# Summing the four partial modulation rows on TensorE and adding their bias on ScalarE

## The chip, the cores and the metric

One core of a Trainium2 chip runs the whole program. The metric is the device time of one execution in microseconds (us). The engines are TensorE (PE, with its weight loads as PEld), VectorE (DVE), ScalarE (ACT), GpSimd (POOL) and SyncE (SP); SP and ACT issue most DMAs from their queues. Each engine carries out its own instructions in program order and waits on semaphores for the others.

## The reference, cut to what matters

Two layers of a hybrid block. Each is steered by six modulation vectors of 1024 per stream (`l` the latents, `c` the context), which come out of one product of a conditioning vector with `w_mod`:

```python
silu_c = jax.nn.silu(c)
silu_cc = jax.nn.silu(c_ctx)
for i in range(DEPTH):            # 2 layers
    ...
    mod_l = jnp.split((silu_c @ w_mod[i] + b_mod[i])[:, None, :], 6, axis=-1)
    mod_c = jnp.split(silu_cc @ w_mod[i] + b_mod[i], 6, axis=-1)
    h_l = modulate(rmsnorm(x, norm_mix_g[i]), mod_l[0], mod_l[1])
    ...
    y_l, y_c = hybrid_mixer(h_l, h_c, p, ctx_out)
    x = x + mod_l[2] * y_l
    x = x + mod_l[5] * expert_choice_ffn(modulate(rmsnorm(x, norm_ffn_g[i]), mod_l[3], mod_l[4]), ...)
    ...
```

`w_mod` is 1024 x 6144 in each layer. `hybrid_mixer` has four branches (attention, an SSD scan, an S5 scan, a short convolution) with gates; `expert_choice_ffn` has 16 experts.

## The kernel before

The 6144 columns of a layer are taken in 24 chunks of 256, so there are 48 chunks in all. `mods` makes one chunk at a time. The contraction of 1024 is split over four column groups of TensorE: the 8 products of L191 leave four partial sums in one PSUM bank (`ps`), group q on rows 32q and 32q+1, one row for each stream. ScalarE copies the bank to `row` in SBUF (L194). What follows is finishing work:

- Two transposes by TensorE (L199) put the chunk's 256 columns onto the partitions, in the first half of a second PSUM bank (`pb`, seen as `pt`).
- VectorE adds the four partial sums (L201, a reduction into `modT`) and then the bias `bmT` (L202).
- Chunks of the parts 2 and 5 are gate chunks, 16 of the 48. The gates are also wanted as rows in DRAM (`mrow`). For them a product with `sel` (L206), a 128 x 32 matrix whose column s has ones on the rows 32q+s, adds the partial sums as rows into the other half of the same bank (`pr`). It is written after L201 in the program, and writes the bank that L201 reads. A DMA from ACT's queue brings the bias rows into `br` (L208; one buffer only, so it waits until the store before has read it), VectorE adds them (L209), for part 5 it also halves them (L212), and SP's queue stores the result to `mrow` (L213).
- Chunks of the parts 1 and 4 make `a_mix` or `a_ffn` by VectorE (L219). This stays.

`mods` is called in the mixer's normalisation (chunks 0 to 7 of layer 0, L355), and in `branches`: as a side generator of the filler work that `main` makes (chunks 8 to 23 of layer 0 and 0 to 7 of layer 1 in layer 0; chunks 16 to 23 of layer 1 in layer 1), and in a run of its own for chunks 8 to 15 of layer 1 (L395). The dense products of the filler (L98 to L100, on `hH`, `hL`, `fwH`, `fwL`) and these chunks share the PSUM banks called `psmm`. The branches SSD and S5 have chains of short steps on DVE, POOL, ACT and PE in banks called `psa` and `psb`; a scheduler interleaves filler and chains by priority, once, when the program is built. At run time each engine's order is fixed. The part of S5's chain that matters here: VectorE builds powers and tables (L986 to L991, into `lo`, `hi`, `Cx`, `z`), then for each group it runs a scan (L1176), combines it into `g` and `S` (L1183 to L1187), and TensorE multiplies that (L1192, L1194).

Of the kernel before, what the change touches and what calls it, by code (L numbers as in the profile page):

```python
# [15 lines left out]
OP = mybir.AluOpType  # L16
# [12 lines left out]
# columns of the packed constants  # L29
# [8 lines left out]
# columns of a layer's packed small parameters  # L38
# [20 lines left out]
class Kern:  # L59
    def __init__(self, ctx, tc, I, out):  # L60
        self.ctx, self.tc, self.nc, self.I, self.out = ctx, tc, tc.nc, I, out
        self.uid = 0
        self.early, self.wafter = (2, 7), {}
        # the experts' weight slots past the early ones: the pools they lie in, bottom up, and the order of first use
        self.lay = ((6, 4, 1, 1), (4, 3, 2, 3))
        self.turn = ([2] + [0] * 6 + [3] + [1] * 4, [2] * 2 + [0] * 4 + [3] * 3 + [1] * 3)

    # ---------------------------------------------------------------- small helpers
# [9 lines left out]
    def psum(self, a, b, mm):  # L78
        """the PSUM banks: for two chains of steps and for the dense products"""
# [6 lines left out]
    def va(self, n, tag=None):  # L86
        """a PSUM bank for a branch's chain of steps"""
# [3 lines left out]
    def pa(self, n):  # L91
        """a PSUM bank for the dense products"""
        return self.va(n, "mm")
# [8 lines left out]
    def split(self, pool, tag, shape, x, bufs=None):  # L102
        """x in two parts that fp32r products carry"""
# [13 lines left out]
    def rsqrt(self, pool, out, x, scale, eps, n, short=False):  # L117
        """out = (x * scale + eps) ** -0.5 on [128, n]"""
# [18 lines left out]
    def constants(self, pool, first, last):  # L137
        """a run of the packed constants"""
# [5 lines left out]
    # ---------------------------------------------------------------- set-up  # L144
    def setup(self):
# [29 lines left out]
        # the experts' inputs and affinities, by layer and stream  # L175
# [3 lines left out]
    def mods(self, l, js, pool=None):  # L179
        """chunks of 256 of layer l's adaLN rows: modT [128, part*8, stream]; the gates' rows to DRAM.  # L180
        Four column groups take two of the eight contraction blocks each"""
# [4 lines left out]
        for j in js:  # L186
# [8 lines left out]
            yield  # L195
            pb = self.pa(512)
            pt = pb[:, :256].rearrange("p (b q c) -> p b q c", b=2, q=4)
            for b in range(2):
                nc.tensor.transpose(pt[:, b].rearrange("p q c -> p (q c)"), row[:, b * 128:(b + 1) * 128], self.ident)  # L199
            mv = modT[:, 2 * j:2 * j + 2]  # L200
            nc.vector.tensor_reduce(mv, pt[:, :, :, 0:2].rearrange("p b q s -> p b s q"), axis=AX.X, op=OP.add)  # L201
            nc.vector.tensor_add(mv, mv, self.bmT[:, l, 2 * j:2 * j + 2, None].to_broadcast([128, 2, 2]))  # L202
            part, jj = divmod(j, 4)
            if part in (2, 5):
                pr = pb[:32, 256:]
                nc.tensor.matmul(pr, self.cst["sel"], row, start=True, stop=True, skip_group_check=True)  # L206
                br = st.tile([2, 256], F32, name="br", tag="br", bufs=1)
                nc.scalar.dma_start(br, I["bmr"][l, part // 3, :, jj * 256:(jj + 1) * 256])  # L208
                nc.vector.tensor_add(br, br, pr[:2])  # L209
                if part == 5:  # L210
                    # the experts' hidden values come twice: halved here
                    nc.vector.tensor_scalar(br, br, 0.5, None, op0=OP.mult)  # L212
# [10 lines left out]
    # ---------------------------------------------------------------- weights and dense products  # L223
    def fraw(self, src, n, pool=None):
        """half of the contraction blocks of a chunk of weights"""
# [4 lines left out]
    def wload(self, src, k, n, extra=None):  # L230
        """weights src [k*128, n] split to fp32r parts: a list of blocks; more columns may be appended"""
# [28 lines left out]
    def cm(self, w, m, o, n):  # L260
        """channel-major product: [128 channels (m-th of the chunk), tokens o..o+n]"""
# [5 lines left out]
    def tm(self, w, t, n):  # L267
        """token-major product: [128 tokens of tile t, n columns]"""
# [5 lines left out]
    # ---------------------------------------------------------------- mixer  # L274
# [21 lines left out]
    def wchunks(self, l):  # L296
        """the experts' weights in the order of use, a quarter of a matrix at a time"""
        n = 0
        for e in range(16):
            for nm in ("w_exp_gate", "w_exp_up", "w_exp_down"):  # L300
                for h in range(4):
# [4 lines left out]
                    if (l, e, nm) == (1, 15, "w_exp_down"):  # L306
                        # the last products go by quarters of the columns
# [10 lines left out]
    def norm(self, l):  # L318
        nc, L0 = self.nc, l == 0
        with self.pool("np") as np_:  # L320
# [24 lines left out]
            if L0:  # L345
                rows = []
                for q in range(5):
                    if q == 3:
                        # the first products take each block as soon as it is there
# [53 lines left out]
    def gate(self, b, mc):  # L403
        """tanh of half a quarter of a branch's gates, kept in DRAM"""
# [10 lines left out]
    def merge(self, l):  # L415
        """the sum of the gated branches onto the residual, then the experts' inputs, tile by tile"""
# [6 lines left out]
        # the experts' weights: the first slots are there from here on, the others once the mixer is done  # L423
# [6 lines left out]
        with self.pool("mg") as mg, ExitStack() as right:  # L430
            mH, mL = (mg.tile([128, 8, W], F32R, name="m" + p) for p in "HL")
            with self.pool("ya") as ya, self.pool("mrg") as mp:
                merged = mp.tile([128, 8, W], F32, name="merged")

                def lower(n):
                    """the lower parts of all but the last n sums"""
# [65 lines left out]
            def add(w, t, c):  # L502
                """a quarter of the columns of a tile"""
# [17 lines left out]
            # the router works on the rows before they are normalised and modulated: its weights take the scale,  # L521
            # the shift gives a row of its own
# [62 lines left out]
    # ---------------------------------------------------------------- short convolution  # L585
# [9 lines left out]
    def pos(o):  # L595
        """column of token o in the padded layout"""
        return o + 1 if o < 256 else o + 3

    def conv(self, dst, xp, w, b):
        """dst[:, i] = w0 x[i] + w1 x[i+1] + w2 x[i+2] (+ b), 770 wide"""  # L600
# [34 lines left out]
    # ---------------------------------------------------------------- SSD  # L635
    def ssd(self):
# [3 lines left out]
        # half the convolution's weights, for silu(y) = (tanh(y/2) + 1) * y/2  # L640
# [42 lines left out]
        # step sizes  # L683
        v = wp.tile([128, NT, 2, 8], F32, name="dtv", tag="dt0")
        for hf, ex in ((1, C_DT), (0, None)):
            w = self.win(C_Z + hf * 256, 256, ex)
            for t in range(NT):
# [7 lines left out]
                if t in self.tiles:  # L695
                    # z, silu'd (twice)
# [929 lines left out]
```

## Time and profile before

| | |
|---|---|
| time, median of 3 runs | 3142.2 us (3141.09 to 3142.49) |
| span of the profiled execution | 3138.9 us |
| its own time | given by its span; the median of the timed runs lies 3.3 us above |
| TensorE busy | 2878.1 us, 92% |
| VectorE busy | 1600.4 us, 51% |
| ScalarE busy | 789.8 us, 25% |
| GpSimd busy | 547.0 us, 17% |

The span runs from the first to the last instruction that the profiler recorded on the one core; the timed runs also hold what lies around it. The busy shares are means over stages with different limits.

### The profile page before, as it was taken

The page shows a single profiled execution, that of the slowest core. Times are in us where ns is not written, and L with a number is a line of the kernel's source. Part 1 is how long each engine was busy: PE and PEld are TensorE (multiplying, and loading weights), DVE is VectorE, ACT ScalarE, POOL GpSimd, SP SyncE. Part 2 cuts the span into 40 slices and gives each one's busy share as a digit, 9 for nine tenths or more (in the row PEclk, how much of TensorE's full clock was granted, in tenths as well). Part 3 has the DMA queues.
Part 4 walks back from the last instruction along what each step waited for, and adds up shares of the span by engine and source line. Part 5 has one row for each costly group of instructions (what it writes and reads, how often), then busy time and mean ns, then how long its engine had stood idle before and what let it go on. Part 6 is the DMA issues. An engine that isn't in the chain of part 4 may idle for free. (4 is left out here: it accounts for less than half of the span.)

```text
span 3138.9 us, 47411 instructions
## 1 busy us (share of the span) xinstructions
PE 2878.1 (92%) x18866; PEld 1863.1 (59%) x18866; DVE 1600.4 (51%) x3581; ACT 789.8 (25%) x1733; POOL 547.0 (17%) x623
## 2 busy tenths in 40 slices
PE   7999888999999979999999799977999996998887
PEld 4866766787788944444443476756686785332223
DVE  5467688555326652323232546798865565232223
ACT  4253222335422200000000332322435421000001
POOL 1022266100004120101000104065210031010001
PEclk9999989999999989999999899988999997999999
DMA  7324433401356369898887541432320486999997
GB/s 235 114 69 133 136 99 121 130 33 35 107 171 207 132 251 384 341 350 342 343 341 280 169 122 54 152 105 74 95 78 18 155 287 252 409 408 409 409 409 302
DMA packets 319615, 648.27 MB, mean 207 GB/s; under 512 B 21409, under 2 KB 190625, under 8 KB 319394
## 3 DMA queue, kind: packets, MB, share of 16 engines
q1 hardware_dynamic: 300688, 601.66, 53.1%
q10 hardware_dynamic: 15186, 32.93, 2.8%
q0 software_dynamic: 3520, 10.65, 0.9%
q8 instruction: 149, 2.44, 0.3%
q14 instruction: 72, 0.59, 0.1%
HBM read 599.71 MB, written 42.32 MB: 205 GB/s over the span
## 5 line engine op out<-in xcount | busy, mean ns | idle before, releaser
L1329 PE MATMUL psa<-we,X 128*64 128x512 f32 (+1 forms) x4096 | 591.8, 492 | 31.1 <-DMA we<-in_w_exp_gate_dram 15.5
L1329 PEld LDWEIGHTS psa<-we,X 128*64 128x64 f32 (+1 forms) x4096 | 203.1, 124 | 394.9 <-issue 285.8
L98 PE MATMUL psmm<-hH,fwH 128*128 128x512 f32 x984 | 373.0, 379 | 8.4 <-DVE xpad L628 3.6
L100 PE MATMUL psmm<-hH,fwL 128*128 128x512 f32 x984 | 368.7, 375 | 0.0
L99 PE MATMUL psmm<-hL,fwH 128*128 128x512 f32 x984 | 367.2, 373 | 0.0
L1359 PE MATMUL psa<-we,hidT 128*64 128x512 f32 x992 | 244.4, 608 | 18.0 <-ACT hidT L1347 11.5
L98 PEld LDWEIGHTS psmm<-hH,fwH 128*128 128x128 f32 x984 | 189.9, 193 | 55.4 <-issue 16.9
L100 PEld LDWEIGHTS psmm<-hH,fwL 128*128 128x128 f32 x984 | 189.9, 193 | 34.7 <-issue 7.8
L99 PEld LDWEIGHTS psmm<-hL,fwH 128*128 128x128 f32 x984 | 189.9, 193 | 31.8 <-issue 6.6
L1340 ACT ACTIVATE hid<-psa 128x512 f32<-128x512 f32 (+1 forms) x48 | 25.3, 526 | 718.3 <-PE psa L1329 574.8
L1364 DVE SCALAR_TENSOR_TENSOR y<-psa,ag,m 64x512 f32<-64x512 f32 x62 | 46.5, 750 | 241.8 <-PE psa L1359 241.0
L1359 PEld LDWEIGHTS psa<-we,hidT 128*64 128x64 f32 x992 | 70.7, 138 | 159.4 <-issue 118.9
L114 DVE TENSOR_TENSOR fwL<-fr,fwH 128x1024 fp32r<-128x1024 f32 (+1 forms) x100 | 115.8, 1159 | 92.9 <-ACT fwH L113 84.0
L1320 POOL TENSOR_TENSOR X<-X,modT 128x512 f32<-128x512 f32 x40 | 41.2, 1042 | 679.2 <-DVE X L1319 679.1
L1342 DVE TENSOR_TENSOR hid<-hid,psa 128x512 f32<-128x512 f32 (+1 forms) x48 | 28.7, 597 | 236.0 <-PE psa L1329 235.7
L465 POOL TENSOR_TENSOR merged<-merged,tgm 128x512 f32<-128x512 f32 (+1 forms) x48 | 62.6, 1323 | 472.3 <-DVE tgm L463 472.0
L113 ACT CAST fwH<-fr 128x1024 fp32r<-128x1024 f32 (+1 forms) x100 | 89.4, 896 | 133.7 <-PE psmm L99 70.3
L98 PE MATMUL psa<-cwH,hH 128*128 128x256 f32 (+1 forms) x432 | 122.4, 284 | 0.2
L100 PE MATMUL psa<-cwH,hL 128*128 128x256 f32 (+1 forms) x432 | 121.7, 282 | 0.0
L99 PE MATMUL psa<-cwL,hH 128*128 128x256 f32 (+1 forms) x432 | 121.4, 281 | 0.0
L1341 DVE SCALAR_TENSOR_TENSOR hid<-hid,psa 128x512 f32<-128x512 f32 (+1 forms) x48 | 28.7, 597 | 165.8 <-ACT hid L1340 165.8
L410 ACT ACTIVATE tg<-psmm 128x512 f32<-128x512 f32 x96 | 50.9, 530 | 169.0 <-PE psmm L100 150.4
(527 smaller groups left out, 5965.8 us busy)
## 6 DMA issues: line engine op xcount, KB each, us to landing
we<-in_w_exp_gate_dram SPq DMA_DIRECT2D x128, 1024.0 KB
we<-in_w_exp_up_dram SPq DMA_DIRECT2D x128, 1024.0 KB
we<-in_w_exp_down_dram SPq DMA_DIRECT2D x128, 1024.0 KB
fr<-in_w_mod_dram SPq DMA_DIRECT2D x96, 512.0 KB
fr<-in_w_in_dram SPq DMA_DIRECT2D x64, 512.0 KB
raw<-in_w_in_dram SPq DMA_DIRECT2D x36, 512.0 KB
gs<-tg ACTq DMA_DIRECT2D x32, 384.0 KB
tgm<-gs SPq DMA_DIRECT2D x32, 384.0 KB
```

Source lines behind the costliest of these rows:

```text
L98: self.nc.tensor.matmul(ps, ah, bh, start=start and i == 0, stop=False)
L99: self.nc.tensor.matmul(ps, ah, bl, start=False, stop=False)
L100: self.nc.tensor.matmul(ps, al, bh, start=False, stop=stop and i == n - 1)
L113: self.nc.scalar.copy(h, x)
L114: self.nc.vector.tensor_sub(l, x, h.bitcast(F32))
L410: nc.scalar.activation(tg[:, o:o + n], self.cm(w, m, o, n), AF.Tanh, scale=0.5)
L465: (V if i == 3 else nc.gpsimd).tensor_add(dst, dst, t)
L1320: nc.gpsimd.tensor_add(X[:, hk], X[:, hk], Bm[:, 24 + h * 4:28 + h * 4, s:s + 1].to_broadcast([128, 4, 128]))
L1329: self.lastup = nc.tensor.matmul(ps[s][j * c:(j + 1) * c], X[s][:, k, r:r + c], w(k)[:, j * n:(j + 1) * n], start=k == 0, stop=k == 7, ski ...
L1341: V.scalar_tensor_tensor(hid, hid, 1.0, g, op0=OP.add, op1=OP.mult)
L1359: nc.tensor.matmul(ps[j * c:(j + 1) * c], lh, w(k)[:, j * n:(j + 1) * n], start=k == 0, stop=k == 7, skip_group_check=True)
L1364: V.scalar_tensor_tensor(Y[s][r, nn], ps[j * c:(j + 1) * c], got[s][1][r, e:e + 1], m5[s][r, nn], op0=OP.mult, op1=OP.mult)
```

## The change

The four partial sums are no longer transposed and then reduced. Two products with `row` as the stationary and the first two columns of `sel` as the moving operand (new L208) transpose and add at once, into 2 x 2 columns of PSUM. ScalarE adds the bias as it moves them into `modT` (new L210, one instruction for each 128 columns). For the gate chunks the product with `sel` (new L204) is followed by a second product into the same place (new L205), 32 columns of the identity's first two rows by `br`, which adds the bias rows; ScalarE then scales by 1 or 0.5 (new L213) into `br`, which SP stores (new L214). The DMA into `br` (new L202) now stands ahead of the products. No instruction of VectorE is left between L194 and `modT` or `mrow`. The diff also takes comments out of the file, which is not shown.

```diff
             row = st.tile([128, 256], F32, name="row", tag="row", bufs=2)
             nc.scalar.copy(row, ps)
             yield
+            part, jj = divmod(j, 4)
             pb = self.pa(512)
-            pt = pb[:, :256].rearrange("p (b q c) -> p b q c", b=2, q=4)
-            for b in range(2):
-                nc.tensor.transpose(pt[:, b].rearrange("p q c -> p (q c)"), row[:, b * 128:(b + 1) * 128], self.ident)
+            pt = pb[:, :4].rearrange("p (b s) -> p b s", b=2)
             mv = modT[:, 2 * j:2 * j + 2]
-            nc.vector.tensor_reduce(mv, pt[:, :, :, 0:2].rearrange("p b q s -> p b s q"), axis=AX.X, op=OP.add)
-            nc.vector.tensor_add(mv, mv, self.bmT[:, l, 2 * j:2 * j + 2, None].to_broadcast([128, 2, 2]))
-            part, jj = divmod(j, 4)
             if part in (2, 5):
-                pr = pb[:32, 256:]
-                nc.tensor.matmul(pr, self.cst["sel"], row, start=True, stop=True, skip_group_check=True)
                 br = st.tile([2, 256], F32, name="br", tag="br", bufs=1)
                 nc.scalar.dma_start(br, I["bmr"][l, part // 3, :, jj * 256:(jj + 1) * 256])
-                nc.vector.tensor_add(br, br, pr[:2])
-                if part == 5:
-                    nc.vector.tensor_scalar(br, br, 0.5, None, op0=OP.mult)
+                pr = pb[:32, 256:]
+                nc.tensor.matmul(pr, self.cst["sel"], row, start=True, stop=False, skip_group_check=True)
+                nc.tensor.matmul(pr, self.ident[:2, :32], br, start=False, stop=True, skip_group_check=True)
+
+            for b in range(2):
+                nc.tensor.matmul(pt[:, b], row[:, b * 128:(b + 1) * 128], self.cst["sel"][:, :2], start=True, stop=True, skip_group_check=True)
+            for b in range(2):
+                nc.scalar.activation(mv[:, b], pt[:, b], AF.Identity, bias=self.bmT[:, l, 2 * j + b:2 * j + b + 1])
+            if part in (2, 5):
+
+                nc.scalar.mul(br, pr[:2], 0.5 if part == 5 else 1.0)
                 nc.sync.dma_start(self.mrow[l, part][:, jj * 256:(jj + 1) * 256], br)
```

On TensorE, at the first gate chunk that falls into layer 0's S5, the order before is this: the two transposes, five dense products of the filler, then the product with `sel`, and more filler.

```order
L100 MATMUL psmm<-hH,fwL 128x256
L199 MATMUL psmm<-cst,row 128x128 x2
L98 MATMUL psmm<-hH,fwH 128x512
L99 MATMUL psmm<-hL,fwH 128x512
L100 MATMUL psmm<-hH,fwL 128x512
L98 MATMUL psmm<-hH,fwH 128x512
L99 MATMUL psmm<-hL,fwH 128x512
L206 MATMUL psmm<-row,cst 32x256
L100 MATMUL psmm<-hH,fwL 128x512
```

At the same place the order after the change is this (L1126 of the changed file is L1125 before, the first product of an S5 group).

```order
L100 MATMUL psmm<-hH,fwL 128x256
L204 MATMUL psmm<-row,cst 32x256
L205 MATMUL psmm<-br,cst 32x256
L208 MATMUL psmm<-cst,row 128x2 x2
L98 MATMUL psmm<-hH,fwH 128x512
L99 MATMUL psmm<-hL,fwH 128x512
L100 MATMUL psmm<-hH,fwL 128x512
L1126 MATMUL psb<-cst,Bx_2746 128x128 x4
L98 MATMUL psmm<-hH,fwH 128x512
```

The chunk's four products now stand together, none of them waits for VectorE, and three dense products follow before S5's first, where before there were seventeen behind the product with `sel`'s wait.

On VectorE, in the second S5 group of layer 0, the order before is this: the steps L1183 to L1187 come twice, with four steps of the gate chunk between them (`fwL` is a weight block of the filler).

```order
L201 TENSOR_REDUCE modT_164<-psmm 128x4
L1185 TENSOR_TENSOR S_2873<-g_2857,g_2858 64x4x95
L1186 TENSOR_TENSOR S_2873<-g_2857,g_2858 64x4x31
L114 TENSOR_TENSOR fwL<-fr,fwH 128x1024
L1187 TENSOR_TENSOR S_2873<-g_2857,g_2858 64x4x64
L202 TENSOR_TENSOR modT_164<-modT_164,bmT 128x4
L209 TENSOR_TENSOR br<-br,psmm 2x256
L1183 TENSOR_TENSOR g_2857<-Vr_2856,Tr_2847 128x384
L1184 TENSOR_TENSOR g_2858<-Vr_2855,Tr_2848 128x384
L212 TENSOR_SCALAR br<-br 2x256
L1185 TENSOR_TENSOR S_2874<-g_2857,g_2858 64x4x95
```

The order after the change is this, with each line number one higher.

```order
L1186 TENSOR_TENSOR S_2873<-g_2857,g_2858 64x4x95
L1187 TENSOR_TENSOR S_2873<-g_2857,g_2858 64x4x31
L1188 TENSOR_TENSOR S_2873<-g_2857,g_2858 64x4x64
L1184 TENSOR_TENSOR g_2857<-Vr_2856,Tr_2847 128x384
L1185 TENSOR_TENSOR g_2858<-Vr_2855,Tr_2848 128x384
L1186 TENSOR_TENSOR S_2874<-g_2857,g_2858 64x4x95
```

The chunk's steps are gone from the chain, and the weight block's step has moved behind it.

## Rows read from the trace of the kernel before

**Rows 1.** The page: span, then each engine's busy time, share and instructions

```profile
span 3138.9 us, 47411 instructions
...
PE 2878.1 (92%) x18866; PEld 1863.1 (59%) x18866; DVE 1600.4 (51%) x3581; ACT 789.8 (25%) x1733; POOL 547.0 (17%) x623
```

**Rows 2.** PE's waits, whole span: total us, times, longest

```profile
PE psb L1157 <- DVE Ur L1151: 20.3, 11, 4.5
PE psmm L206 <- DVE modT L201: 19.2, 6, 5.2
```

**Rows 3.** PE's waits from 370 to 530 us, layer 0's S5

```profile
PE psmm L206 <- DVE modT L201: 13.3, 3, 5.2
```

**Rows 4.** PE's waits from 2040 to 2240 us, layer 1's S5

```profile
PE psb L1157 <- DVE Ur L1151: 13.5, 6, 4.5
...
PE psmm L206 <- DVE modT L201: 5.9, 3, 3.4
```

**Rows 5.** Groups by line and form: count, busy us, mean ns, idle before

```profile
L202 DVE TENSOR_TENSOR modT<-modT,bmT 128x4 f32<-128x4 f32 x48 | 11.6, 242 | 0.9
L201 DVE TENSOR_REDUCE modT<-psmm 128x4 f32<-128x16 f32 x48 | 8.0, 168 | 8.2 <-PE psmm L199 7.8
L212 DVE TENSOR_SCALAR br<-br 2x256 f32<-2x256 f32 x8 | 6.5, 816 | 0.1
L209 DVE TENSOR_TENSOR br<-br,psmm 2x256 f32<-2x256 f32 x16 | 6.5, 404 | 2.4 <-PE psmm L206 2.3
...
L194 ACT COPY row<-psmm 128x256 f32<-128x256 f32 x48 | 17.8, 371 | 46.3 <-PE psmm L191 46.2
...
L719 ACT ACTIVATE ssa<-par 128x16 f32<-128x16 f32 x2 | 0.4, 216 | 0.0
```

**Rows 6.** Windows: length, each engine's busy us, granted clock, DMA share, GB/s

```profile
46.00:370.00 324.00, 313.79 (x1932) 245.89 (x1930) 199.76 (x524) 126.72 (x301) 52.88 (x94) 0.99 0.36 111
...
370.00:530.00 160.00, 131.52 (x992) 99.20 (x985) 135.62 (x259) 38.45 (x90) 102.13 (x88) 0.87 0.33 104
...
2040.00:2240.00 200.00, 159.72 (x1006) 117.98 (x1004) 174.72 (x312) 51.42 (x103) 116.64 (x102) 0.89 0.27 85
```

**Rows 7.** Windows of line L194 alone: length, ACT busy us (count), clock, DMA

```profile
46.00:370.00 324.00, 4.47 (x12) 0.99 0.36 111
...
530.00:620.00 90.00, 1.47 (x4) 0.98 0.42 132
...
1800.00:2040.00 240.00, 2.98 (x8) 1.00 0.36 109
```

**Rows 8.** PE in order of time, 372 to 390: start, us, wait

```profile
373.10 0.38 PE L199 MATMUL psmm<-cst,row 128*128 128x128 f32 x2
...
379.83 1.04 PE L206 MATMUL psmm<-row,cst 128*32 128x256 f32 x2 [5.19 <-DVE modT L201]
...
389.07 0.66 PE L1125 MATMUL psb<-cst,Bx 128*128 128x128 f32 x4 [2.23 <-POOL S L1180]
```

**Rows 9.** DVE in order of time, 404 to 418

```profile
410.37 1.22 DVE L212 TENSOR_SCALAR br<-br 2x256 f32<-2x256 f32 x1
411.52 0.54 DVE L1185 TENSOR_TENSOR S<-g,g 64x380 f32<-64x380 f32 x1
```

**Rows 10.** PE and DVE in order of time, 438 to 457

```profile
445.41 1.06 PE L206 MATMUL psmm<-row,cst 128*32 128x256 f32 x2 [3.28 <-DVE modT L201]
...
451.45 0.82 DVE L986 TENSOR_TENSOR Cx<-PC,cc 128x640 f32<-128x640 f32 x1 [5.30 <-PE psb L1194]
```

**Rows 11.** PE in order of time, at 91 and at 1062

```profile
91.49 0.62 PE L206 MATMUL psmm<-row,cst 128*32 128x256 f32 x2
...
1062.90 1.41 PE L568 MATMUL psa<-wa,hT 128*128 128x16 f32 x12
```

**Rows 12.** DMA issues in order of time, 1763 to 1768

```profile
1763.88 0.36 SPq L213 DMA_DIRECT2D mrow<-br  x1
...
1767.73 0.30 ACTq L208 DMA_DIRECT2D br<-in_bmr_dram  x1
```

## The prediction

> **What bounds the kernel now.** I read the page first: TensorE is busy for 92% of the span and no other engine passes 51% [rows 1]. So I asked what TensorE waits for. Of all its waits the second longest in sum is one that this change takes away: the product L206 waits for VectorE's reduction L201, 6 times, 19.2 us in all [rows 2]. All of that is in two places: 13.3 us in layer 0's S5 and 5.9 us in layer 1's [rows 3, 4]. The windows say what these two places are like [rows 6]. Elsewhere, as from 46 to 370 us, TensorE is busy for 97% of the time at a granted clock of 0.99. In the S5 stretches it is busy for 82% and 80%, its mean clock is only 0.87 and 0.89, and VectorE is busy for 85% and 87%. There VectorE and GpSimd make S5's chain, and TensorE both feeds it and waits for it. The reader should see from this that a wait of TensorE in S5 is worth nothing by itself: it is worth something only where S5's chain stands behind it.
>
> In order of time the first stall shows how it comes about. The transposes L199 ran at 373.10, but L206 only at 379.83, after 5.19 us of idleness [rows 8], since L201 stood behind S5's set-up in VectorE's queue. The two records of L206 then took 1.04 us, and at 91.49, with no stall ahead, they took 0.62 us [rows 8, 11]: TensorE's granted clock had fallen from its upper to its lower level while it was idle.
>
> **What goes from VectorE.** L201, L202, L209 and L212 go, 8.0 + 11.6 + 6.5 + 6.5 = 32.6 us of work [rows 5]. Only what lies on S5's chain counts. L212 stands 8 times, four in each S5. In the chain one of them starts at 410.37 and the next step at 411.52, so it costs 1.15 us [rows 9]; L209 costs some 0.3 of its 0.40 us, L201 and L202 some 0.1 to 0.2 each. A gate chunk's steps on the chain are thus worth 1.7 us.
>
> A rule of the Trainium skill bears on that size: in "SBUF — State Buffer", section "Who interferes with whom", a VectorE `tensor_scalar` may run in a mode that takes the ports which VectorE shares with GpSimd for the whole instruction, and the later of the two blocks. The mean of L212, 0.82 us for 256 columns on two partitions against 0.40 for L209 [rows 5], agrees; by 0.4 us without that blocking the four gate chunks of an S5 would give some 3 us less. ScalarE, the page says, waits for no one there.
>
> **What goes from TensorE's waits.** Four gate chunks of layer 0 fall into S5, and three of them have a stall [rows 3].
> The first stall (5.19 us) is not paid back: S5's first product L1125 waits 2.23 us at 389.07 for GpSimd anyway [rows 8], and GpSimd's work hangs on VectorE's. The filler that TensorE does not get done there is done in a later wait. What counts is the VectorE work: 1.9 us.
> The second is of the same kind, with L212 on a VectorE that has no idle time: 1.7 us.
> The third stall does count: L206 waits 3.28 us and is done at 446.47; behind it stand S5's products L1192 and L1194 at the lower clock, and VectorE idles for 5.30 us until L1194 is done [rows 10]. Without the wait they start some 3 us earlier and run at the upper clock; I take 5 us, since VectorE's idle time bounds it.
> The gate chunk without a stall is worth some 1 us. Layer 0's S5: -9.6 us.
> Layer 1's S5 has 87% of VectorE and shorter stalls [rows 4, 6], so only the chain's VectorE steps count, at 1.7 us for three of the four gate chunks: -5 us. Both ends: none, if GpSimd ends last at each, and 6.8.
> After a stall the clock comes back: where TensorE is the later engine again within S5, I give it -2 us, between 0 and 6 (a third of a gap of some 2 us behind each of the six stalls, and at most half of the 13% and 11% that the mean clocks lack over the parts without other stalls).
>
> **What is added on TensorE.** The two products L208 are in fp32 with 2 moving columns. No such product is in the trace. The nearest are L568's (128 x 16), which leave two records each: 12 records in 1.41 us, so one each 0.11 us and 0.44 us for two products [rows 11]. The transposes took 0.38 us for two, with 0.11 us from one to the next, so 0.22 [rows 8]. The difference is 0.23 us a chunk, 48 x 0.23 = 10.9 us; the lower end is 0, if the two columns make up for the second record. I take the upper, since L206 and L568 both leave two. L205 moves the 256 columns of L206 a second time: two records start 0.24 us apart (0.62 us for both with the last lasting 0.38), so 0.48 us, 16 times, 7.7 us. Of this 18.6 us what lies in TensorE-bound stretches counts: 12 + 4 + 8 = 24 chunks by L194 [rows 7], of which the four of layer 0's part 2 are gate chunks: 24 x 0.23 + 4 x 0.48 = +7.4 us (lower end 2). The others lie in start-up, in S5 and at the head of layer 1, where TensorE waits in any case; without that cover they cost the other 11 us.
>
> **What is added on ScalarE.** 96 times L210 and 16 times L213: nearest L719 at 0.216 and L194 at 0.371 us [rows 5], so 96 x 0.22 + 16 x 0.37 = 27 us on an engine that is busy for 25%. Behind them stand the casts of the filler's weights and, at start-up and at the head of layer 1, the normalised blocks `hH`, which TensorE waits for. L210 waits only for TensorE, as L201 did. I charge +1 us at start-up (between 0 and 3: eight chunks of 0.44 us).
>
> **The wait that is added.** L205 needs `br`, so TensorE now waits for a DMA that has itself waited until the previous gate chunk's store has read `br`; before, only VectorE's L209 waited for that. Queued behind L205 are this chunk's L208, the filler, and S5's products. From the store's issue to the next load's issue took 1763.88 to 1767.73, 3.85 us, at the head of layer 1 [rows 12]; the load's own landing comes on top. In S5 the gate chunks stand a whole group apart, so `br` is there long before. At the head of layer 1 the four come close together, but the new order puts other products between L204 and L205 there. I charge +1 us (between 0 and three times 3.85, 11.6).
>
> **The sum.** -9.6 - 5 - 2 + 7.4 + 1 + 1 = -7.2 us. It is made on the profiled execution, whose span of 3138.9 us lies 3.3 us under the median of 3142.2; I take that part as unchanged, so 3135.0 us, 0.23% faster. About 0.2%, 6.3 us, is what a measurement of this kernel can tell from no change.
>
> **The rivals.**
> *The stalls come back elsewhere.* S5's chain is the bound at the third stall too: TensorE, rid of L206's wait, waits at L1157 (already 20.3 us [rows 2]) or L1194 instead. Then layer 0's S5 gives 1.9 + 1.7 + 1 = 4.6, layer 1's 3, the clock nothing, and the costs of 9.4 us eat it: +1.8 us, 3144. For it speaks VectorE's 85% and 87%; against it the 5.30 us in which VectorE itself waits. No change.
> *The stalls come back in full.* TensorE is what is late in S5 and all filler counts: 19.2 us, 6 us of clock and 5 us of layer 1's chain, less 9.4: 3142.2 - 20.8 = 3121. For it speaks the 92%; against it the low share of TensorE just there.
> *Slower: TensorE waits for `br`.* The store and the load of `br` come in turn with one buffer. Each of the 12 gate chunks that follow another would hold TensorE by up to 3.85 us; at 3 x 3.85 at layer 1's head and 9 x 1.2 in the other places (a third of it, the DMA share being lower there) this is 22 us, so 3135 + 22 = 3157. It decides from 13.5 us on. For it speaks that the load stands in ACT's queue just after the last L213 in several places; against it, that the chunks are a group apart.
> On this the Trainium skill has a rule, in "DMA: Bandwidth & Descriptors", section "Anatomy of one DMA": about 2 us are fixed for each DMA, whatever its size, most of it until the write is confirmed (for DMAs that GpSimd issues). By that the store and the load together take some 4 us, an estimate from that page; this case's 3.85 us for the store alone is longer, and 12 such turns in full would give some 3183.
>
> **How the numbers follow.** My sum: 0.42, with its own range 3130 to 3140, of which 0.26 faster and 0.16 within 0.2%. Stalls elsewhere: 0.20, no change. Stalls in full: 0.22, faster. Waits for `br`: 0.16, slower. Faster 0.48, same 0.36, slower 0.16. The range from 3120 to 3147 leaves out the last case and little else.
>
> **What would show it.** In the changed profile no PE wait names L201, and the 13.3 and 5.9 us are gone. The first S5 window has a mean clock of 0.90 or more and is 8 to 11 us shorter, the second some 5; the window from 46 to 370 grows by 4 to 5 us, that of layer 1's SSD by 2. L208 leaves 192 records at 0.11 us, L205 two at 0.24. Waits of PE for the DMA of `br` stay under 2 us. The prediction is wrong if the S5 windows keep their length with longer waits at L1157 or L1194 (then VectorE's chain was the bound throughout), if PE waits for `br` in more than a few microseconds, or if the added products cost other than 0.23 and 0.48 us.

## The result, and the profile after

The change made the kernel slower: 3167.3 us (median of 4 runs, 3160.9 to 3170.6) against 3142.3 us, a ratio of 1.0075 with a 95% interval of 1.0060 to 1.0089. The prediction was 3135, 0.23% faster.

The page of the changed kernel first (span, then busy time, share and instructions of each engine).

```profile
span 3168.7 us, 47636 instructions
...
PE 2917.8 (92%) x18994; PEld 1892.8 (60%) x18994; DVE 1579.6 (50%) x3461; ACT 813.3 (26%) x1845; POOL 542.7 (17%) x623
```

VectorE's busy time fell by 20.8 us, though the four lines that went had 32.6 [rows 5], and ScalarE's rose by 23.5 of the 27 foreseen. TensorE's busy time rose by 39.7 us over [rows 1], twice the 18.6 us of added products, and its idle time, span less busy, fell only from 260.8 to 250.9 us. A second profile of the same program, taken later ("Start-up or later" below), with a span of 3153.4 us, tells which part of this is steady:

```profile
PE 2902.3 (92%) x18994; PEld 1881.5 (60%) x18994; DVE 1580.4 (50%) x3461; ACT 813.6 (26%) x1845; POOL 546.1 (17%) x623
```

Its mean granted clock is 0.969, where the first profile has 0.963 and the kernel before 0.968. TensorE is busy for 24.2 us more than before and idle for 9.8 us less; the other 15 us of the first profile's busy time are a lower clock in that one execution.

PE's waits over the whole span (total us, times, longest):

```profile
PE psb L1158 <- DVE Ur L1152: 26.8, 9, 4.5
PE psb L1195 <- DVE S L1188: 18.8, 7, 4.2
...
PE psmm L205 <- DMA br<-in_bmr_dram: 1.8, 2, 1.0
```

The wait for L201, 19.2 us in [rows 2], is gone as the change says. Its neighbour L1157 (here L1158), 20.3 us before, has 26.8. The wait for `br` that could have made a slower kernel is 1.8 us.

The same for the stretch from 370 to 600 us, layer 0's S5, first of the kernel before:

```profile
PE psmm L206 <- DVE modT L201: 13.3, 3, 5.2
PE psb L1157 <- DVE Ur L1151: 6.8, 5, 3.1
PE psb L1194 <- DVE S L1187: 3.3, 4, 2.5
```

and of the changed one:

```profile
PE psb L1158 <- DVE Ur L1152: 12.6, 4, 4.1
PE psb L1195 <- DVE S L1188: 7.9, 3, 4.2
PE psb L1126 <- POOL S L1181: 6.5, 1, 6.5
```

The three sum to 23.4 us before and to 27.0 after (23.7 in the second profile). The stalls have moved to S5's own steps.

What is new is at the start. PE in order of time in the kernel before (start, us); each L191 group is half or all of a chunk's products, x8 or x16 records:

```profile
14.20 1.08 PE L191 MATMUL psmm<-fr,cpad 128*32 128x256 f32 x8 [14.20 <-DVE rs_t L124]
...
21.68 1.07 PE L191 MATMUL psmm<-fr,cpad 128*32 128x256 f32 x16
...
25.00 0.64 PE L191 MATMUL psmm<-fr,cpad 128*32 128x256 f32 x8
...
62.45 0.85 PE L678 MATMUL psa<-cst,bc 128*128 128x128 f32 x6
```

and in the changed one:

```profile
18.12 1.01 PE L208 MATMUL psmm<-cst,row 128*128 128x2 f32 x4
...
22.54 1.93 PE L191 MATMUL psmm<-fr,cpad 128*32 128x256 f32 x16
...
38.80 1.08 PE L191 MATMUL psmm<-fr,cpad 128*32 128x256 f32 x8
...
47.01 0.72 PE L191 MATMUL psmm<-fr,cpad 128*32 128x256 f32 x8
...
70.92 0.84 PE L679 MATMUL psa<-cst,bc 128*128 128x128 f32 x6
```

A group of 8 lasts 1.08 us at the lower of TensorE's two clocks and 0.64 at the upper. Before, TensorE is at the upper one from about 22 us on; now it is at the lower one until 47, although it is idle for less time: up to 42 us its longest gap is 0.55 us, before it was 1.48. SSD's first transposes come at 70.92 and not at 62.45: 8.5 us of the loss are there at this point. (The granted-clock column of the windows says 1.00 for this stretch in both, so I go by durations.)

The windows of [rows 6] after (length, busy us of PE, PEld, DVE, ACT, POOL, clock, DMA):

```profile
46.00:370.00 324.00, 314.15 (x1930) 244.56 (x1929) 184.90 (x455) 132.78 (x330) 48.90 (x92) 0.98 0.37 110
370.00:530.00 160.00, 135.42 (x995) 102.71 (x993) 136.55 (x255) 41.43 (x103) 100.21 (x89) 0.90 0.36 112
2040.00:2240.00 200.00, 167.01 (x1061) 125.79 (x1059) 161.28 (x321) 56.16 (x116) 106.34 (x92) 0.89 0.32 99
```

They begin at other places of the work than before, by 5 to 9 us in the first two and by 26 in the last. The S5 window's clock rose from 0.87 to 0.90 as I said it would, but S5 did not get shorter: from the first L1125 to the first L1218, 385.1 to 570.0 before, it took 184.9 us, and now 196.2 (188.9 in the second profile). Layer 1's took 192.9 us before and 195.5 and 195.3 now.

At a gate chunk of the changed kernel (PE in order of time):

```profile
97.86 0.62 PE L204 MATMUL psmm<-row,cst 128*32 128x256 f32 x2
98.40 0.61 PE L205 MATMUL psmm<-br,cst 2*32 2x256 f32 x2
98.95 0.61 PE L208 MATMUL psmm<-cst,row 128*128 128x2 f32 x4
99.42 0.48 PE L98 MATMUL psmm<-hH,fwH 128*128 128x512 f32 x1
```

L205 takes 0.55 us from start to start, and L208 takes 0.47 behind it (0.36 where no gate product stands ahead, at 252 and 272 us), where L199 took 0.14 before the next product started. With 0.55 + 0.33 us for each of the 16 gate chunks and 0.23 for each of the other 32, 21 us are added.

### The profile page after: what moved, and what is told of

It reads as the page before. It is cut to its first block, busy times and chain, and to the rows that moved or that the text cites. A ratio compares the mean times of both kernels' runs of the same rounds, so it can differ in the third digit from the quotient of the medians.

```text
span 3168.7 us, 47636 instructions
## 1 busy us (share of the span) xinstructions
PE 2917.8 (92%) x18994; PEld 1892.8 (60%) x18994; DVE 1579.6 (50%) x3461; ACT 813.3 (26%) x1845; POOL 542.7 (17%) x623
## 5 line engine op out<-in xcount | busy, mean ns | idle before, releaser
L466 POOL TENSOR_TENSOR merged<-merged,tgm 128x512 f32<-128x512 f32 (+1 forms) x48 | 62.3, 1316 | 470.5 <-DVE tgm L464 307.4
L961 ACT COPY PT<-psa 128x256 f32<-128x256 f32 (+1 forms) x144 | 63.4, 478 | 113.3 <-PE psa L960 113.3
```

What stands on the lines that cost most here:

```text
L466: (V if i == 3 else nc.gpsimd).tensor_add(dst, dst, t)
L961: nc.scalar.copy(PT[hh][:, k0 // 128:(k0 + n) // 128].rearrange("p a t -> p (a t)"), pp)
```

## The experiments

All times are medians; ratios are to the kernel before on the same chip, with 95% intervals.

**What the parts cost.** The change, with each summing product moving 128 columns, the last two of them those of `sel`:

```diff
-            pt = pb[:, :4].rearrange("p (b s) -> p b s", b=2)
+            pt = pb[:, :256].rearrange("p (b s) -> p b s", b=2)
...
-                nc.tensor.matmul(pt[:, b], row[...], self.cst["sel"][:, :2], ...)
+                nc.tensor.matmul(pt[:, b], row[...], self.cst["wide"], ...)   # ident[:, 2:], sel[:, :2]
-                nc.scalar.activation(mv[:, b], pt[:, b], ...)
+                nc.scalar.activation(mv[:, b], pt[:, b, 126:], ...)
```

> The change, but each product that sums and transposes moves 128 columns (126 columns of the identity and then the two of sel) in place of 2; ScalarE reads the last two. Theory A (the 2-column products leave TensorE at its lower clock): the start-up's L191 groups reach 0.64 us by 25 us as before, not at 47, the stretches at the lower clock together fall from 138 to about 100 us, and the time to 3140 to 3150. Theory B (the added products and the extra hop over ScalarE cost the time whatever their width): as the change or slower, 3162 to 3172, since no product is taken away and each moves more.

Measured 3154.8 us, 1.0039 (1.0027 to 1.0051), 12.5 us under the change, and the intervals do not touch. TensorE moves 64 times as many columns in these products and the kernel is faster. I counted the stretches of over 1 us in which dense products and L191 last as at the lower clock (0.63 us for 512 columns, 0.42 for 256): about 92 us before, 138 with the change, 97 here, from one profile each (the change's is the one with the lower clock of its two). That is what theory A expects; the time stayed above its 3140 to 3150. The 12.5 us are not the width alone: the scheduler places the filler otherwise with 128 columns, and TensorE's order parts from the change's at the first dense products.

The gate half alone (`L204`, `L205`, ScalarE's scaling; `modT` by transposes and VectorE):

```diff
-            for b in range(2):
-                nc.tensor.matmul(pt[:, b], row[...], self.cst["sel"][:, :2], ...)
-            for b in range(2):
-                nc.scalar.activation(mv[:, b], pt[:, b], AF.Identity, bias=...)
+            for b in range(2):
+                nc.tensor.transpose(pt[:, b], row[...], self.ident)
+            nc.vector.tensor_reduce(mv, ...)
+            nc.vector.tensor_add(mv, mv, self.bmT...)
```

> The gate half of the change alone: rows by the product with sel, bias rows by the second product, scaling by ScalarE; modT by transposes and VectorE as before. Theory A (2-column products and the clock): no such product is left, so 3132 to 3146. Theory B (added products on the path): of 18.6 us of added products 7.7 stay, so about a third of the loss of 25 us, 3148 to 3153. Theory C (TensorE waits for br): most of the loss stays, 3160 or more.

Measured 3154.6 us, 1.0034 (1.0020 to 1.0048). Theory A's upper end of 3146 fails for this half; the time is a little over theory B's range and under C's.

The other half alone (2-column products and ScalarE's bias; the gate rows' bias and halving by VectorE, L206 ahead):

```diff
-                nc.tensor.matmul(pr, self.ident[:2, :32], br, ...)
...
-                nc.scalar.mul(br, pr[:2], 0.5 if part == 5 else 1.0)
+                nc.vector.tensor_add(br, br, pr[:2])
+                if part == 5:
+                    nc.vector.tensor_scalar(br, br, 0.5, None, op0=OP.mult)
```

> The other half alone: modT by the 2-column products and ScalarE; the gates' rows by the product with sel ahead of them, bias and halving by VectorE as before. Theory A: the start-up stays at the lower clock until about 47 us and the time is 3158 or more. Theory B: 10.9 of 18.6 us of added products stay, about 3157. Theory C (br): 3140 or less.

Measured 3173.6 us, 1.0095 (1.0078 to 1.0112): theory A's side; B's 3157 and C fall. The start-up was at the lower clock until 25 us and again from 34 to 46. The two halves do not add up to the whole: 12 + 31 against 25 us. In the profiles most of these 18 us are idle time of TensorE (span less busy): 264.8 us in the gate half and 262.3 in this one, 260.8 before, and 250.9 in the whole change. Each half keeps two of VectorE's four steps. The whole change, which keeps none, has 10 us less idle time than the kernel before, and so has its version with the bias on VectorE (250.8, below). That these steps are the reason was not tried by itself, and the scheduler's order is another one in each version.

**What the stalls were worth.** The kernel before with L206 ahead of the transposes:

```diff
+            if part in (2, 5):
+                pr = pb[:32, 256:]
+                nc.tensor.matmul(pr, self.cst["sel"], row, start=True, stop=True, ...)
             pt = pb[:, :256]...
...
-                pr = pb[:32, 256:]
-                nc.tensor.matmul(pr, self.cst["sel"], row, start=True, stop=True, ...)
```

> The kernel before, with only the product L206 moved ahead of the transposes, so that it no longer waits for VectorE's reduction. If the 19.2 us of waits are worth what the prediction gave them without VectorE's part and without added products: 5 to 8 us less, 3134 to 3137. If S5's chain of VectorE is the bound throughout: 3140 to 3143.

Measured 3138.8 us, 0.9986 (0.9973 to 1.0000): some 3.6 us, between the two expectations, with an interval that reaches no change. Its PE waits:

```profile
PE psb L1158 <- DVE Ur L1152: 28.9, 12, 4.1
PE psb L1195 <- DVE S L1188: 24.1, 10, 4.9
```

Of the 19.2 us that went, 8.6 are back at L1158 [rows 2] and 8.5 at L1195 (15.6 us before). TensorE's idle time is 260.8 us as before, so the rival "the stalls come back elsewhere" is shown without any added product. Layer 0's S5 took 187.5 us in this profile, no less than the 184.9 before, and layer 1's took 187.6 (192.9 before).

At the place of the third stall, for which the prediction took 5 us, VectorE's wait of 5.30 us [rows 10] is 0.68 here, and L1195 runs at the upper clock. But the time is not kept: the next step that TensorE waits for is L1158, where it had waited 0.30 us before. First the kernel before:

```profile
458.26 0.30 PE L1157 MATMUL psb<-Ur,Bt 128*64 128x96 f32 x1 [0.30 <-DVE Ur L1151]
```

and with L206 ahead:

```profile
441.01 0.86 DVE L987 TENSOR_TENSOR Cx<-PC,cc 128x640 f32<-128x640 f32 x1 [0.68 <-PE psb L1195]
...
452.21 0.34 PE L1158 MATMUL psb<-Ur,Bt 128*64 128x96 f32 x1 [4.10 <-DVE Ur L1152]
```

The same, with the halving by ScalarE (`nc.scalar.mul(br, br, 0.5)` for L212):

> The kernel before with the product L206 ahead of the transposes, and the halving of part 5 by ScalarE in place of VectorE; nothing is added on TensorE. If VectorE's 1.15 us for each halving lie on S5's chain: some 4 to 7 us under the version with L206 ahead alone, 3132 to 3135. If TensorE's sum of work is the bound: no difference, 3137 to 3141.

Measured 3136.1 us, 0.9975 (0.9965 to 0.9985): faster than the kernel before beyond its interval, and the best version tried. Beside the one without this step the intervals overlap; the medians differ by 2.7 us, of the 4 to 7 expected. In its profile L1158 waits 22.6 us and L1195 23.3, TensorE's idle time is 258.8 us, and layer 0's S5 took 187.8 us and layer 1's 187.9.

**What added products cost.** L206 ahead, both transposes and L206 done twice:

```diff
-                nc.tensor.matmul(pr, self.cst["sel"], row, start=True, stop=True, ...)
+                for _ in range(2):
+                    nc.tensor.matmul(pr, self.cst["sel"], row, start=True, stop=True, ...)
...
-            for b in range(2):
+            for b in (0, 1, 0, 1):
                 nc.tensor.transpose(pt[:, b], row[...], self.ident)
```

> The kernel before with L206 ahead of the transposes, and both the transposes and the product with sel done twice, which adds 48 x 0.22 + 16 x 0.48 = 18 us of products, as many as the change adds, none of them of 2 columns. Theory that added products count in full: 3139 + 18 = 3155 to 3160. Theory of the prediction (7.4 of 18.6 us count, the others lie in waits): 3144 to 3148. Theory that all of the loss is the clock: 3139.

Measured 3157.3 us, 1.0039 (1.0022 to 1.0056): 18.5 us over the version with L206 ahead, for 18 us of products. The two were measured on different chips; by their ratios the difference is 17 us, give or take 7 (an estimate from the two intervals). So the products count in full or nearly so, and the prediction's 7.4 of 18.6, which would have given 3146, falls. The ten runs lie 20 us apart, the longer ones at the lower mean clock (0.964 to 0.967 above 3160 us, 0.968 to 0.971 below 3152), so a part of any one difference is the clock's. TensorE's idle time is 257.3 us, 3.5 less than with L206 ahead: the added products found hardly a wait to lie in.

L206 twice in the gate chunks alone, on the version with ScalarE's halving (the same `for _ in range(2)`, and nothing else):

> L206 ahead of the transposes and the halving by ScalarE, with the product L206 done twice in each of the 16 gate chunks: 16 x 0.48 = 7.7 us of products added, as many as the second product of the gate half adds, but none that waits for br. If products count in full and nothing else is in the loss of the gate half: about 3136 + 8 = 3144, and some 8 us of the gate half's 3154.6 are then something else. If 3150 or more: the products and the places the scheduler gives them explain the gate half alone.

Measured 3153.9 us, 1.0033 (1.0011 to 1.0055), 18 us for 7.7 us of products (8.8 at the 0.55 measured). So the gate half's time appears without `br` in a product, and some 9 us in it are no product's time. What they are is open. The filler was put elsewhere: from the first L1218 to layer 0's first router product, 492.9 us before, it takes 509.5 here and 509.3 in the gate half, with 80 more records of products, and S5 holds 433 dense products in place of 453. But this is no mark of the gate half: the doubled version (507.2) and the change with 128 columns everywhere (509.0) show the same shift, and the change itself does not (492.1). Some of the 9 us may be the clock, whose mean over the ten runs is 0.966, against 0.968 in the version without the doubling.

**The wait for br.** The gate half, with the finished row written into `row[:2]`, so that `br` need not wait for the store:

```diff
-                nc.scalar.mul(br, pr[:2], 0.5 if part == 5 else 1.0)
-                nc.sync.dma_start(self.mrow[...], br)
+                nc.scalar.mul(row[:2], pr[:2], 0.5 if part == 5 else 1.0)
+                nc.sync.dma_start(self.mrow[...], row[:2])
```

> The gate half alone, but ScalarE writes the finished gate row into the first two partitions of row, and the store reads it there, so that br is free for the next load as soon as the second product has read it and no longer waits for the store. If waits for br cost the gate half its part that the products don't explain: some 5 to 8 us less than 3154.6, 3146 to 3150. If not: 3152 to 3157.

Measured 3150.9 us, 1.0023 (1.0013 to 1.0033). It lies between the two expectations and its interval overlaps the gate half's: unclear, at most a few microseconds. The waits for `br` in the two profiles of the change, 1.8 and 2.3 us, say the same.

**ScalarE's bias.** The change, with one addition by VectorE in place of L210's two:

```diff
-            for b in range(2):
-                nc.scalar.activation(mv[:, b], pt[:, b], AF.Identity, bias=...)
+            nc.vector.tensor_add(mv, pt, self.bmT[:, l, 2 * j:2 * j + 2, None].to_broadcast([128, 2, 2]))
```

> The change, with the bias of modT added by VectorE, reading PSUM, in one instruction, in place of ScalarE's two. If the hop over ScalarE at start-up (two steps of 0.2 us, and VectorE's a_mix behind them) and ScalarE's order matter: 2 to 6 us less than the change's 3167, 3161 to 3165. If ScalarE's share is hidden, as theories A and B have it: the change's time within its spread, 3164 to 3171.

Measured 3166.4 us, 1.0068 (1.0050 to 1.0086), the change's own time. Which engine adds the bias makes no difference that these runs can tell.

**The start-up's clock.** The change, with transposes and VectorE in the first eight chunks (`if pool is not None` around the old lines):

> The change, with the first eight chunks of layer 0 (the start-up) by transposes and VectorE as before. Theory A (2-column products leave TensorE at its lower clock): the start-up's L191 groups are at 0.64 us from about 25 us on, SSD's first transposes at 62 to 63 us and not at 70.6, and the time falls by some 8 us to 3157 to 3161. Theory B (added products only): by at most the 1.8 us of the eight chunks' products, 3164 to 3168.

Measured 3160.2 us, 1.0063 (1.0040 to 1.0086), 7 us under the change, as theory A has it, though the intervals overlap. SSD's first transposes come at 62.3 us.

The version with L206 ahead, with the 2-column products and ScalarE's bias in the first eight chunks only:

> The kernel before with L206 ahead of the transposes, and only the first eight chunks of layer 0 by the 2-column products and ScalarE. Theory A (clock): the start-up stays at the lower clock for 10 to 25 us longer, SSD's first transposes come at 67 to 71 us and not at 62, and the time is 5 to 9 us over that with L206 ahead alone, 3144 to 3148. Theory B: 0 to 2 us over it, 3138 to 3141.

Measured 3144.5 us, 1.0004 (0.9994 to 1.0014), 5.7 us over the version with L206 ahead, though the intervals overlap. The same with 128 columns in those products:

> As the version with the 2-column products in the first eight chunks only, but these products move 128 columns; the order of TensorE's instructions up to the first dense product is the same. Theory A (the width of the products sets the clock): the start-up is at the upper clock by about 25 us, the stretch up to SSD's first transposes falls from 51 to 44 or 46 us, and the time from 3144.5 to about 3139. If the low clock of the start-up came from the hop over ScalarE or from chance: 51 us and 3144 to 3146 as with 2 columns.

Measured 3141.6 us, 0.9998 (0.9986 to 1.0009). The interval overlaps that with 2 columns, so the medians do not decide. The profiles do: TensorE's order up to the first dense product differs by one transpose. With 2 columns:

```profile
32.96 1.53 PE L346 MATMUL psa<-cst,xh 128*128 128x128 f32 x6 [1.42 <-DVE hf L350]
34.43 1.08 PE L191 MATMUL psmm<-fr,cpad 128*32 128x256 f32 x8
35.44 1.02 PE L205 MATMUL psmm<-cst,row 128*128 128x2 f32 x4
...
69.86 0.85 PE L686 MATMUL psa<-cst,bc 128*128 128x128 f32 x6
```

and with 128:

```profile
32.78 0.89 PE L348 MATMUL psa<-cst,xh 128*128 128x128 f32 x6 [1.42 <-DVE hf L352]
33.60 0.64 PE L193 MATMUL psmm<-fr,cpad 128*32 128x256 f32 x8
34.17 0.71 PE L207 MATMUL psmm<-cst,row 128*128 128x128 f32 x4
...
64.99 0.85 PE L688 MATMUL psa<-cst,bc 128*128 128x128 f32 x6
```

Both had been at the upper clock for the groups before, and both have the same gap of 1.42 us. Only the version with 2 columns is at the lower clock behind it: its group of 8 takes 1.08 us in place of 0.64, and SSD's first transposes come 4.9 us later.

All 17 profiles of this case, one or two of each version, bear this out. In the eleven whose first eight chunks use transposes or 128 columns, no L191 group takes 1.08 us after 25 us, and SSD's first transposes come at 61.5 to 65.8 us. In the six with 2 columns there, one of them without ScalarE's step, TensorE is still or again at the lower clock at 44 us, and the transposes come at 69.0 to 72.9. The three with 128 columns (64.3 to 65.8) are some 2 to 3 us behind those with transposes, so of the 8.5 us some 5 to 7 go with the width (4.9, 5.7 and 6.6 in the three pairs), and the rest with what else the change adds there.

**Start-up or later.** Three kernels on one chip: the change, the change with 128 columns in the first eight chunks only, and with 128 columns in the forty later ones only (`w = 128 if pool is not None else 2`, and the reverse).

> The change itself, beside the next two on the same chip: 3161 to 3171, start-up at the lower clock beyond 40 us.

> The change, with 128 columns in the summing products of the first eight chunks only. If the width of the start-up's products is what costs there: SSD's first transposes at 63 to 65 us and not at 70.9, and 5 to 8 us less than the change. If not: no difference.

> The change, with 128 columns in the summing products of the 40 later chunks, and 2 in the first eight. If the width matters after start-up too (the all-wide version took 12.5 us less than the change, of which the start-up explains 5 to 8): 4 to 7 us less than the change. If only the start-up's matter: no difference.

Measured 3165.1 us, 1.0085 (1.0068 to 1.0102); 3160.0 us, 1.0055 (1.0035 to 1.0075); 3156.2 us, 1.0056 (1.0039 to 1.0073). The medians gain 5 and 9 us, but both intervals overlap the change's. For the start-up the profiles settle it again (SSD's first transposes at 71.57 in the change and at 65.84 with 128 columns, a little later than the 63 to 65 expected). For the later chunks a single profile doesn't, since the clock there differs from run to run. The mean granted clock, which does not show the start-up, is 0.964 over the 24 runs of the six versions with 2 columns in the later chunks (0.961 to 0.969) and 0.967 over the 12 runs of the two with 128 (0.964 to 0.968). So the clock is the higher one there, but the order of the filler changes with the width too, and how much of the gain is the width's stays open. Only the two parts together are clear of the change's interval.

The change's second profile shows where its runs' spread of 16 us comes from. It is the same program with the same order on TensorE, with a span 15.3 us shorter than the first, and the difference lies in the clock. A window in layer 1's SSD in the first profile (length, busy us, clock):

```profile
1990.00:2008.00 18.00, 17.17 (x63) 10.68 (x62) 11.35 (x39) 5.84 (x16) 2.60 (x6) 0.62 0.32 97
```

and the window 10 us earlier, with about the same work, in the second:

```profile
1980.00:1998.00 18.00, 17.18 (x93) 11.32 (x92) 15.08 (x48) 7.87 (x21) 3.04 (x6) 1.00 0.35 102
```

TensorE is equally busy in both and gets through 63 records of products in one and 93 in the other. This place makes some 6 of the 15.3 us; layer 0's S5 makes 7 more.

## Why the prediction was wrong

Three terms of the sum failed:

1. **The added products**, "12 + 4 + 8 = 24 chunks ... +7.4 us". The differences of unit prices nearly held: L205 takes 0.55 us for 0.48 foreseen, and L208 takes 0.22 us more than the transposes (0.36 and 0.14, where the prediction had 0.44 and 0.22), or 0.33 behind a gate product. What failed is the rule that only those in TensorE-bound stretches count. Products that double existing ones cost 17 to 18.5 us for 18, while TensorE's idle time fell by 3.5 us. The filler is a fixed amount of work, so a product that is added where TensorE also waits can push a dense product out to where it does not; in the doubled version 101 more records of products than with L206 ahead alone stand between layer 0's S5 and its router. The prediction named the other 11 us as the price "without that cover", and there was hardly any.

2. **TensorE's clock**, of which the prediction spoke as something that only stalls cost. The 2-column products were costed by their time alone. With them TensorE stays at its lower clock at start-up, or falls back to it behind a gap that the wide version gets over, and this is some 5 to 7 of the 8.5 us that are lost there. With 128 columns in place of 2 everywhere the time is 12.5 us less in all, the order's part included. "I charge +1 us at start-up" was a term for the right place with the wrong cause: with the bias on VectorE in place of ScalarE's hop the time was the same.

3. **The removed stalls and VectorE's steps**, -9.6 - 5 - 2. L206 put ahead takes the waits away with nothing added, and gave 3.6 us; with the halving moved off VectorE it is 6 to 7 (L201, L202 and L209 still stand in that version, by the prediction 0.5 to 0.7 us a chunk). The rival "stalls come back elsewhere", at 0.20, had it: the waits reappear at L1158 and L1195, and TensorE's idle time stays at 260.8 us. Of the two S5 stretches layer 1's got 5 us shorter, as the prediction had it, and layer 0's, with the larger term, did not get shorter at all (187.5 and 187.8 us for 184.9, one profile each). At the third stall VectorE's idle time went as foreseen, and TensorE then waited 4.10 us at L1158 in place of 0.30.

Of the two rules weighed ahead, that of the Trainium skill in "DMA: Bandwidth & Descriptors", section "Anatomy of one DMA", did not come to bear: by the 4 us a turn that were estimated from it the loss would have been in waits for `br`, and they are 1.8 us. The one of the Trainium skill in "SBUF — State Buffer", section "Who interferes with whom", agrees with the kernel before. Three of the eight L212 met no instruction of GpSimd and took 0.28 us; five met one that was running, and ended 0.14 to 0.15 us after it, four of them after 1.22 to 1.26 us. The GpSimd step that the L212 at 410.37 [rows 9] met, and an L212 that met none:

```profile
410.05 1.40 POOL L986 TENSOR_TENSOR Tr<-hi,lo 128x384 f32<-128x384 f32 x1 [6.03 <-DVE g L1183]
...
438.64 0.28 DVE L212 TENSOR_SCALAR br<-br 2x256 f32<-2x256 f32 x1
```

What the time gains by it is not shown: moving the halving to ScalarE gave 2.7 us by the medians, within the intervals.

Right were that ScalarE's work is hidden, and that TensorE hardly waits for `br` (1.8 us; +1 charged). The sum as it now stands goes by medians of single versions: 3142.3 - 3.6 (stalls) = 3138.8 with L206 ahead; + 16.0 to the all-wide change at 3154.8, which holds the 21 us of added products, VectorE's gain and the order's part; + 12.5 for the 2 columns and the order that goes with them = 3167.3. That the steps add up so is by construction. Shown by a run of its own are the price of added products (the doubled ones), what the stalls were worth (L206 ahead) and the clock at start-up (the pair and the 17 profiles). Open are the 9 us of the gate half beyond its products, how the 12.5 us divide between the width, the clock and the order of the filler, and why the halves cost 18 us more than the whole.

## What to carry to other kernels

On a kernel whose filler is a fixed amount of work, expect a product that is added to the bounding engine to cost its full time, also where that engine waits, and a stall that is removed inside a chain that another engine bounds to give little. Before a wide product is replaced by one of a few columns that does the same, look what the clock does behind it: time a group of unchanged products before and after. Take a second profile of the same program before a few microseconds are read into one.

## What was not expected of the hardware

- fp32 products with 2 and with 128 moving columns take about the same time: a chunk's two took 0.47 us up to the next product's start behind a gate product and 0.36 behind a dense one, in the change (98.95 to 99.42, 252.22 to 252.58) and in the all-wide version alike. Making them narrow saved nothing here.
- A TensorE that issues 2-column products between its other work stayed at its lower clock for 33 us (14 to 47) in both profiles of the change, with no gap above 0.56 us up to 42 us. With wide ones in the same places it was at the upper clock by about 23 us in all three profiles, with gaps of up to 1.42 us.
- Two profiles of one program differ by 15.3 us, with the same order of TensorE's instructions and the same idle time (250.9 and 251.1 us, span less busy). At one place, 6 us of the difference, the lower clock came in at 1993 and held for 14 us in one of them, and did not in the other.
